# The recurrence's gates of a hybrid layer on one Trainium2 core: 128-row products one tile at a time, and 64-row products two tiles at a time

## The chip, the core and the metric

The kernel runs on one core of a Trainium2 chip. The metric is the device time of one execution in microseconds. The core's engines have their own instruction queues, each worked off in order: PE (TensorE) multiplies, ACT (ScalarE) evaluates functions, DVE (VectorE) does the elementwise work, POOL (GpSimd) a little of it, and SP (SyncE) issues most transfers. They meet only through semaphores.

## What is computed

The reference is one layer with three token mixers beside each other, for 512 positions of width 1024 in float32: a gated MLP (branch A), sparse attention with compressed keys (branch B) and a gated linear recurrence (branch C). The change is about branch C, about the projection that B's compression reads, and about the order in which gates of the merge are made.

```python
xc = conv4(xr) + conv_b                       # causal, per channel
xh = xc.reshape(B, S, 16, 64)                 # 16 heads of 64 channels
r = sigmoid(einsum('bshi,hio->bsho', xh, w_a) + b_a)
i = sigmoid(einsum('bshi,hio->bsho', xh, w_x) + b_x)
log_a = -8 * r * softplus(-lam)
a = exp(log_a)
b_in = sqrt(-expm1(2 * log_a)) * (i * xc)
h[t] = a[t] * h[t-1] + b_in[t]                # scan over positions
y_c = h * gelu(gate)
...
merged = g0 * (y_a @ w_br_a) + g1 * (y_b @ w_br_b) + g2 * (y_c @ w_br_c)
```

Everything behind (output projection, two norms, a SwiGLU block) is the same in both kernels.

## The kernel before

**Tiles.** Activations lie transposed, channels on the 128 partitions and the 512 positions along the row. A tile is 128 output channels of a projection. Float32 accuracy comes from halves: `split` (L131 on ACT, L136 on DVE) writes a rounded copy `hi` and then the rest `lo = x - hi`, and a product is hi*hi + hi*lo + lo*hi. A projection tile is thus 8 blocks of channels x 3 = 24 matmuls of 128x512 into one PSUM bank (`passes`, L263); a `yield` after each six lets other work be placed between them.

**Weights.** `wload` brings the weights of a tile through two raw buffers and has them split, in the order of `wlist`. The split of a coming tile is issued as the current one starts, so it stands on ACT and DVE between whatever else these two engines have in their queues; PE waits for it if it is late.

**Branch C.** `xr_tile(b, c)` (L488) makes one of two batches of four tiles: the projection, the convolution (L499 and L501, `xc`), the halves `ch` and `cl` of `xc`, and then the gates: for each of R and I three matmuls of 128x512 (L509), against block-diagonal weights `wab` that hold two heads of 64 channels, in a bank of the kind "tr". ACT reads R with a sigmoid (L511) and I with a tanh (L514), 128x512 each, and DVE makes (tanh + 1) * xc of it (L515). PSUM has six banks "mm" and two "tr". Once the four tiles of a batch are there, `rec_batch(b)` (L517) takes a tanh of R per tile (L523, T), one square root over the four (L524), four exponentials (L530), and per tile two multiplications on DVE (L539, L540) and the scan (L542). Sigmoid and tanh, root, and exponential lie in different tables of ACT, hence the two ACT_TABLE_LOAD of a batch. `rg_tile` makes the gelu gate of a tile (L451 to L454), `rec_out` (L556 and on) multiplies it in and splits the result into `ych` and `ycl`.

**The rest of the stretch.** `cmp_tile` makes the keys and values that B compresses, `compress` multiplies them (L784 first, then L800 or L814, with the tanh L793 between), `gate_tile` (L712 to L722) makes B's 48 gates and transposes them, and `c_gate(j)` (L1179) is a projection tile with a tanh for the merge of branch C. `c_stage` makes that merge: sums of y_c are split (the tiles named t, L131 and L136), and `b_pair` multiplies halves of weights and sums (L1273, 128x256 each), with its partial results copied out of the banks by ACT.

**What sets the order.** The work is written as generators. `run(main, side, rate)` steps through the tiles of `main` and advances `side` at the given rate; what a tile yields as a number is how many steps later its rest (the gates, say) is continued, in the list `late`. A scheduler places instructions on each engine in about this order, and `tc.issue_after(x)` keeps an instruction behind x. Around the change the main order is: the value tiles and compression tile 0; four input tiles of the first batch and the gate tile; four gelu tiles, compression tile 1 and four input tiles of the second batch, with the first batch's recurrence beside them; then a gelu tile (as fifth of the list), three more, compression tiles 2 and 3, branch gate 0, the first compression, branch gate 1, with the second batch beside them; then `c_stage`.

Of the kernel before, what the change touches and what calls it, by code (L numbers as in the profile page):

```python
# [52 lines left out]
def hybrid_block(ctx: ExitStack, tc: tile.TileContext, A, out):  # L53
# [89 lines left out]
    def w_in(*tiles):  # L143
# [5 lines left out]
    w_in(*range(T_XR + 1, T_XR + 8, 2), T_CMP + 1, *range(T_XR + 8, T_XR + 16, 2), *range(T_XR + 9, T_XR + 16, 2),  # L149
         T_CMP + 2, T_CMP + 3)  # L150
# [306 lines left out]
    wab = {}  # L457

# [5 lines left out]
    def load_wab():  # L464
        raw = wab["raw"]
        hi = slab("wabh", F32R, "wab", (2, NK, 128), 48)
        lo = slab("wabl", F32R, "wab", (2, NK, 128), 48)
        wab["hi"], wab["lo"] = hi, lo
        for _ in range(4):
            yield  # L470
        for k in range(0, NK, 2):
            split(raw[:, :, k:k + 2], hi[:, :, k:k + 2], lo[:, :, k:k + 2])
            yield
# [14 lines left out]
    def xr_tile(b, c):  # L488
        if c == 0:
            res["late"] = res["raw"]  # L490
            rec[b] = dict(R=slab("r", tag="y" if b else "m"), GG=slab("gg", tag="m"), TI=slab("ti", tag=("s0", "s1")[b]))
# [11 lines left out]
        ch, cl = row("ch", F32R), row("cl", F32R)  # L503
        split(xc, ch, cl)
        yield 4
        for g, dst in ((0, "R"), (1, "TI")):
            pg = bank("tr")
            for t, (w, x) in enumerate((("hi", ch), ("hi", cl), ("lo", ch))):
                PE.matmul(pg, wab[w][:, g, k, :], x, start=(t == 0), stop=(t == 2))  # L509
            if g == 0:  # L510
                SC.activation(rec[b]["R"][:, c, :], pg, AF.Sigmoid, bias=vec[:, V_BA + k:V_BA + k + 1])  # L511
            else:
                ti = rec[b]["TI"][:, c, :]
                last = SC.activation(ti, pg, AF.Tanh, scale=0.5, bias=half[:, 0, k:k + 1])  # L514
                res["ti"] = last, V.scalar_tensor_tensor(ti, ti, 1.0, xc, op0=OP.add, op1=OP.mult)  # L515
            yield

    def rec_batch(b):
        r = rec[b]
        r["T"] = slab("t", tag="s2")  # L520
        for c in range(4):
            k = 4 * b + c
            SC.activation(r["T"][:, c, :], r["R"][:, c, :], AF.Tanh, scale=sp4[:, k:k + 1])  # L523
        root = SC.activation(r["T"], r["T"], AF.Sqrt, scale=1.0 / 16)  # L524
# [182 lines left out]
    def gate_tile():  # L707
# [11 lines left out]
        yield  # L719
# [610 lines left out]
    def c_stage(first):  # L1330
# [20 lines left out]
        run([c_gate(2), hidden(second), c_gate(3)], begin(), 1.5)  # L1351
# [697 lines left out]
    def run(main, side=None, rate=1.0):  # L2049
# [3 lines left out]
        late = []  # L2053
# [212 lines left out]
```

## Time and profile before

| | us |
|---|---|
| median of 3 runs (1089.49 to 1089.56) | 1089.54 |
| the profiled execution | 1089.44 |
| its span, first to last instruction | 1087.7 |
| around the span | 1.74 |
| PE busy | 1078.3 (99%) |
| DVE busy | 883.0 (81%) |
| ACT busy | 661.7 (61%) |
| granted TensorE clock, mean | 0.998 |

PE is pipelined: a matmul of 128x512 is shown with 0.39 us, but the next one starts 0.227 us later, so start times count and not durations. On ACT and DVE, too, an instruction starts a little before the one ahead of it has ended. A row of the chain or of a timeline gives the start in the span, the length, the engine, and the line; "x4" stands for four in a row, and what is in square brackets is the idle time before it and what ended it. The stretch with the gate products lies between 66 and 147 us, the merge of branch C begins at 211 us.

### The profile page before, as it was taken

How to read it: one execution, taken by the hardware profiler on the slowest of the kernel's cores; microseconds unless marked ns; L12 is line 12 of the kernel's file. 1: busy time of each engine (PE TensorE's matmuls, PEld its weight loads, DVE VectorE, ACT ScalarE, POOL GpSimd, SP SyncE). 2: the span in 40 equal slices, each digit the busy share in tenths (PEclk: the TensorE clock that was granted, in tenths of full speed). 3: DMA queues.
4: the chain of work that ended last, by engine and by line, in shares of the span. 5: the costliest groups of instructions: out<-in, count | busy, mean ns of one | idle time of the engine just before them, and what ended most of it. 6: DMA issues, size and time to landing. Idle time of an engine off the chain costs nothing.

```text
span 1087.7 us, 16765 instructions
## 1 busy us (share of the span) xinstructions
PE 1078.3 (99%) x6450; PEld 948.5 (87%) x6450; DVE 883.0 (81%) x1557; ACT 661.7 (61%) x1210; POOL 29.0 (3%) x41
## 2 busy tenths in 40 slices
PE   9999999999999999999999999999999999999997
PEld 7888888999889888898888889988999999998886
DVE  6967779669675899998998887876988888889675
ACT  6757574454444676876777655555666666667542
POOL 0000000000000000000000000000000000022200
PEclk9999999999999999999999999999999999999999
DMA  8332325430322221102111134271323322378902
GB/s 312 113 99 82 97 86 204 178 98 20 117 78 78 78 59 39 59 20 79 59 39 59 58 118 136 72 257 39 117 78 117 117 104 97 130 227 202 191 20 97
DMA packets 35312, 115.07 MB, mean 106 GB/s; under 512 B 3584, under 2 KB 3984, under 8 KB 34336
## 3 DMA queue, kind: packets, MB, share of 16 engines
q1 hardware_dynamic: 28496, 97.01, 27.0%
q0 software_dynamic: 5152, 11.09, 5.0%
q10 hardware_dynamic: 1584, 5.90, 1.4%
q8 instruction: 50, 0.82, 0.3%
q14 instruction: 30, 0.25, 0.1%
HBM read 111.89 MB, written 2.10 MB: 105 GB/s over the span
## 4 chain that ended last, share of the span: by engine, by line
PE 97%; DVE 1%; DMA 0%; issue 0%; ACT 0%; DVEq 0%; SPq 0%; ACTq 0%
PE mm L263 37%; PE mm L1755 18%; PE mm L1273 7%; PE mm L1894 6%; PE mm L625 4%; PE mm L1509 4%; PE o L992 4%; PE sc L954 3%; PE tr L979 3%; PE tr L1894 3%; PE mm L870 2%; PE tr L784 1%; PE tr L509 1%; PE mm L1611 1%; PE tr L685 1%; PE tr L892 1%
## 5 line engine op out<-in xcount | busy, mean ns | idle before, releaser
L263 PE MATMUL mm<-hh,hi 128*128 128x512 f32 x504 | 199.5, 396 | 0.0
L263 PE MATMUL mm<-hh,lo 128*128 128x512 f32 x504 | 197.4, 392 | 0.0
L263 PE MATMUL mm<-hl,hi 128*128 128x512 f32 x504 | 196.9, 391 | 0.0
L136 DVE TENSOR_TENSOR lo<-raw,hi 128x1024 fp32r<-128x1024 f32 (+1 forms) x105 | 121.0, 1153 | 38.4 <-ACT hi L131 35.3
L131 ACT ACTIVATE hi<-raw 128x1024 fp32r<-128x1024 f32 (+1 forms) x105 | 105.3, 1003 | 46.5 <-PE mm L263 17.3
L263 PEld LDWEIGHTS mm<-hh,lo 128*128 128x128 f32 x504 | 94.6, 188 | 19.7
L263 PEld LDWEIGHTS mm<-hl,hi 128*128 128x128 f32 x504 | 94.7, 188 | 18.4 <-issue 0.2
L263 PEld LDWEIGHTS mm<-hh,hi 128*128 128x128 f32 x504 | 94.7, 188 | 18.0 <-PE mm L1273 0.2
L960 ACT ACTIVATE P<-P,ast 128x128 f32<-128x128 f32 (+3 forms) x128 | 70.7, 555 | 23.1 <-DVE ast L958 22.5
L958 DVE CUSTOM_DVE_ANT_0 P<-sc,mask 128x128 f32<-128x128 f32 (+3 forms) x128 | 57.9, 484 | 8.2 <-PE sc L954 7.3
L131 ACT ACTIVATE ph<-tr 128x512 fp32r<-128x512 f32 x80 | 46.9, 592 | 25.9 <-PE tr L979 24.0
L136 DVE TENSOR_TENSOR pl<-tr,ph 128x512 fp32r<-128x512 f32 x80 | 54.4, 685 | 2.7 <-PE o L992 0.9
L954 PE MATMUL sc<-K,q 128*128 128x512 f32 (+2 forms) x192 | 51.0, 368 | 0.0
L1755 PE MATMUL mm<-t,hi 128*128 128x256 f32 x288 | 50.7, 276 | 0.0
L1894 PE MATMUL mm<-hi,u 128*128 128x512 f32 x160 | 50.1, 389 | 0.0
L979 PE MATMUL tr<-ident,P 128*128 128x128 f32 x320 | 48.7, 273 | 0.0
L979 PEld LDWEIGHTS tr<-ident,P 128*128 128x128 f32 x320 | 39.0, 140 | 9.8 <-DVE pl L136 1.0
L136 DVE TENSOR_TENSOR lo<-bs,hi 128x1024 fp32r<-128x1024 f32 x28 | 34.1, 1220 | 11.6 <-ACT hi L131 11.6
L1755 PEld LDWEIGHTS mm<-t,hi 128*128 128x128 f32 x288 | 43.4, 188 | 0.0
L1755 PE MATMUL mm<-fh,hi 128*128 128x256 f32 x144 | 40.0, 278 | 0.0
L1755 PE MATMUL mm<-fh,lo 128*128 128x256 f32 x144 | 39.8, 276 | 0.0
L1755 PE MATMUL mm<-fl,hi 128*128 128x256 f32 x144 | 39.8, 276 | 0.0
(489 smaller groups left out, 2896.6 us busy)
## 6 DMA issues: line engine op xcount, KB each, us to landing
raw<-in_w_in SPq DMA_DIRECT2D x64, 512.0 KB, 3.5
rawp<-in_w_fi SPq DMA_DIRECT2D x20, 1024.0 KB, 5.1
bs<-in_w_fo POOLq DMA_DIRECT2D x20, 512.0 KB, 8.1
raw<-in_w_br SPq DMA_DIRECT2D x14, 512.0 KB, 3.6
w<-in_cw ACTq DMA_DIRECT2D x4, 1024.0 KB, 6.7
raw<-in_w_o SPq DMA_DIRECT2D x8, 512.0 KB, 4.1
bs<-in_w_fo SPq DMA_DIRECT2D x8, 512.0 KB, 8.0
raw<-in_w_v SPq DMA_DIRECT2D x6, 512.0 KB, 4.9
```

The costliest lines, as they stand in the source:

```text
L131: res["hi"] = SC.activation(hi, src, AF.Copy)
L136: res["lo"] = V.tensor_sub(lo, src, f32(hi))
L263: res["mm"] = PE.matmul(ps[:m, n0:n1], w[:, k * 128:k * 128 + m], x[k][:, n0:n1], start=(t == 0), stop=(t == 3 * NK - 1))
L625: res["mm"] = PE.matmul(b[c], x[k][:, c * 128:(c + 1) * 128], w[:, kk * 512:kk * 512 + 512], start=(k == 0 and t == 0), stop=(k == NK - 1 ...
L954: PE.matmul(ps[:, :w * n].rearrange("p (b n) -> p b n", b=w), lhs, K[:, i, brs[0]:brs[-1] + 1, :n], start=(i == 0), stop=(i == 1))
L958: V.tensor_tensor_reduce(out=t, in0=ps[:, b * n:b * n + n], in1=mask[0][:, S - n:], scale=-0.125, scalar=3.0e38, op0=OP.add, op1=OP.min, a ...
L960: SC.activation(t, t, AF.Exp, scale=-1.0, bias=st[:, 0, j, b:b + 1], accum_out=st[:, 1, j, b:b + 1])
L979: PE.transpose(pt[:, j * 128:(j + 1) * 128], self.part(j, br)[:, kt * 128:(kt + 1) * 128], ident)
L992: PE.matmul(po, VV[:, kt, g % 2, br].rearrange("p i d -> p (i d)"), x, start=(br == 0 and kt == 0 and t == 0), stop=(br == 1 and kt == a a ...
L1273: res["mm"] = PE.matmul(ps, u[:, k * 128:k * 128 + 128], v[:, k], start=(start and k == t == 0), stop=(k == 3 and t == 2), skip_group_chec ...
L1755: res["mm"] = PE.matmul(ps, w[:, k * 128:k * 128 + 128], x[:, k], start=(start and k == t == 0), stop=(k == 3 and t == 2), skip_group_chec ...
L1894: PE.matmul(ps, a, b, start=id(ps) not in begun, stop=i == len(ops) - 1, skip_group_check=True)
```

## The change

**Weights of the gates.** `load_wab` now lays `wab` out as, for each tile and each half of 64 partitions, 64 columns of R's head and 64 of I's. One matmul of 64 rows and 128 columns makes R and I of one head: R's 64 channels in the bank's rows 0 to 63, I's in rows 64 to 127.

**Two tiles at a time.** `xr_tile` leaves the gates to the second tile of each pair (c odd). Four banks "mm" are taken, one for each tile and half. In three rounds (hi*ch, lo*ch, hi*cl) four matmuls follow each other (L519), the pair's second tile first, the two halves in turn; they are held in this order with `issue_after`. That is 12 matmuls of 64 rows for a pair, 48 in all, as many as before. ACT reads each bank in 64x512: four sigmoids (L525) and four tanhs (L526) for a pair, where it was two and two of 128x512. The rows `ch` and `cl` use buffers of other kinds.

**Second pair of a batch.** After its sigmoids come the tanhs of T (L535, L536), the tanhs of the first tile's I, and then `rec_batch` is begun: the root (L550), then the exponentials (L556). The last tile's two tanhs of I are kept behind the root by `issue_after`. The list `late` is handed from one `run` to the next, so that the second pair's gates stand within the first tiles of the next stage; `gated` lets the recurrence wait for both pairs.

**Order of tiles.** Compression tile 2 moves ahead, to the end of the second batch's input tiles, and the gelu tiles of that batch follow all four together; the list of weights is changed to match. Branch gates 0 and 1 stand ahead of the first compression, gates 2 and 3 ahead of the second, where one of the two stood between. `gate_tile` continues its transposes two steps later.

The core of the diff:

```diff
@@ -148,4 +148,4 @@
     wlist.append((A["w_gate"], "gate"))
-    w_in(*range(T_XR + 1, T_XR + 8, 2), T_CMP + 1, *range(T_XR + 8, T_XR + 16, 2), *range(T_XR + 9, T_XR + 16, 2),
-         T_CMP + 2, T_CMP + 3)
+    w_in(*range(T_XR + 1, T_XR + 8, 2), T_CMP + 1, *range(T_XR + 8, T_XR + 16, 2), T_CMP + 2, *range(T_XR + 9, T_XR + 16, 2),
+         T_CMP + 3)
 
@@ -457,2 +457,3 @@
     wab = {}
+    ends = slice(0, 64), slice(64, 128)
 
@@ -465,4 +466,4 @@
         raw = wab["raw"]
-        hi = slab("wabh", F32R, "wab", (2, NK, 128), 48)
-        lo = slab("wabl", F32R, "wab", (2, NK, 128), 48)
+        hi = slab("wabh", F32R, "wab", (NK, 128), 48)
+        lo = slab("wabl", F32R, "wab", (NK, 128), 48)
         wab["hi"], wab["lo"] = hi, lo
@@ -470,5 +471,7 @@
             yield
-        for k in range(0, NK, 2):
-            split(raw[:, :, k:k + 2], hi[:, :, k:k + 2], lo[:, :, k:k + 2])
-            yield
+        for o in ends:
+            for i in range(2):
+                g = slice(64 * i, 64 * i + 64)
+                split(raw[o, i, :, o], hi[o, :, g], lo[o, :, g])
+                yield
 
@@ -490,3 +493,3 @@
             res["late"] = res["raw"]
-            rec[b] = dict(R=slab("r", tag="y" if b else "m"), GG=slab("gg", tag="m"), TI=slab("ti", tag=("s0", "s1")[b]))
+            rec[b] = dict(gates=0, R=slab("r", tag="y" if b else "m"), GG=slab("gg", tag="m"), TI=slab("ti", tag=("s0", "s1")[b]))
         k = 4 * b + c
@@ -502,16 +505,43 @@
         yield
-        ch, cl = row("ch", F32R), row("cl", F32R)
+        ch, cl = row("ch", F32R, "tg"), row("cl", F32R, "q32")
         split(xc, ch, cl)
-        yield 4
-        for g, dst in ((0, "R"), (1, "TI")):
-            pg = bank("tr")
-            for t, (w, x) in enumerate((("hi", ch), ("hi", cl), ("lo", ch))):
-                PE.matmul(pg, wab[w][:, g, k, :], x, start=(t == 0), stop=(t == 2))
-            if g == 0:
-                SC.activation(rec[b]["R"][:, c, :], pg, AF.Sigmoid, bias=vec[:, V_BA + k:V_BA + k + 1])
-            else:
-                ti = rec[b]["TI"][:, c, :]
-                last = SC.activation(ti, pg, AF.Tanh, scale=0.5, bias=half[:, 0, k:k + 1])
-                res["ti"] = last, V.scalar_tensor_tensor(ti, ti, 1.0, xc, op0=OP.add, op1=OP.mult)
-            yield
+        rec[b]["x"] = rec[b].get("x", []) + [(k, xc, ch, cl)]
+        yield 5 if c == 3 else 3
+        if c % 2 == 0:
+            return
+        two = rec[b].pop("x")
+        pg = [[bank("mm") for _ in ends] for _ in two]
+        for t in range(3):
+            for i, (k, xc, ch, cl) in reversed([*enumerate(two)]):
+                w, x = (("hi", ch), ("lo", ch), ("hi", cl))[t]
+                for n, own in enumerate(ends):
+                    with tc.issue_after(res["gate"].ins) if t or n or not i else nullcontext():
+                        res["gate"] = PE.matmul(pg[i][n], wab[w][own, k, :], x[own], start=(t == 0), stop=(t == 2))
+        yield
+        r = rec[b]
+
+        def act(out, part, k, own, n):
+            if part == 0:
+                return SC.activation(out[own], n[:64], AF.Sigmoid, bias=vec[own, V_BA + k:V_BA + k + 1])
+            return SC.activation(out[own], n[64:], AF.Tanh, scale=0.5, bias=half[own, 0, k:k + 1])
+
+        for i, (k, xc, ch, cl) in enumerate(two):
+            for n, own in enumerate(ends):
+                act(r["R"][:, k % 4, :], 0, k, own, pg[i][n])
+            if c == 3:
+                if i == 0:
+                    r["T"] = slab("t", tag="s2")
+                    for j in range(2):
+                        SC.activation(r["T"][:, j, :], r["R"][:, j, :], AF.Tanh, scale=sp4[:, 4 * b + j:4 * b + j + 1])
+                SC.activation(r["T"][:, k % 4, :], r["R"][:, k % 4, :], AF.Tanh, scale=sp4[:, k:k + 1])
+        for i, (k, xc, ch, cl) in enumerate(two):
+            ti = r["TI"][:, k % 4, :]
+            for n, own in enumerate(ends):
+                with tc.issue_after(r["root"].ins) if "root" in r else nullcontext():
+                    last = act(ti, 1, k, own, pg[i][n])
+            res["ti"] = last, V.scalar_tensor_tensor(ti, ti, 1.0, xc, op0=OP.add, op1=OP.mult)
+            if c == 3 and i == 0:
+                r["rec"] = rec_batch(b)
+                next(r["rec"])
+        r["gates"] += 1
 
@@ -519,7 +549,3 @@
         r = rec[b]
-        r["T"] = slab("t", tag="s2")
-        for c in range(4):
-            k = 4 * b + c
-            SC.activation(r["T"][:, c, :], r["R"][:, c, :], AF.Tanh, scale=sp4[:, k:k + 1])
-        root = SC.activation(r["T"], r["T"], AF.Sqrt, scale=1.0 / 16)
+        root = r["root"] = SC.activation(r["T"], r["T"], AF.Sqrt, scale=1.0 / 16)
 
@@ -718,3 +744,3 @@
         SC.activation(s[:64], s[:64], AF.Sigmoid)
-        yield
+        yield 2
         pt = bank("tr")
@@ -1350,3 +1376,3 @@
 
-        run([c_gate(2), hidden(second), c_gate(3)], begin(), 1.5)
+        run([c_gate(2), c_gate(3), hidden(second)], begin(), 1.5)
         more = seq(second, gmlp_prep(), v_norm())
@@ -2048,3 +2074,3 @@
 
-    def run(main, side=None, rate=1.0):
+    def run(main, side=None, rate=1.0, late=None, keep=False):
 
@@ -2052,3 +2078,3 @@
         credit = 0.0
-        late = []
+        late = late or []
         for m in main:
@@ -2069,4 +2095,4 @@
             credit += rate
-        for _, m in late:
-            for _ in m:
+        while late and not keep:
+            for _ in late.pop(0)[1]:
                 pass
@@ -2075,2 +2101,3 @@
                 pass
+        return late
 
@@ -2124,12 +2151,16 @@
     run([v_half(0), v_half(1), cmp_tile(0)], seq(norm(), load_wab()))
-    run(xr_tiles(0, gate_tile()))
-    tiles = xr_tiles(1, rg_tile(1, 0))
-    run(four(rg_tile, 0) + [cmp_tile(1)] + tiles[:4], rec_batch(0), 0.45)
+    late = run(xr_tiles(0, gate_tile()), keep=True)
+    tiles = xr_tiles(1, cmp_tile(2))
+
+    def gated(b):
+
+        while rec[b]["gates"] < 2:
+            yield
+        yield from rec[b]["rec"]
+
+    late = run(four(rg_tile, 0) + [cmp_tile(1)] + tiles[:4], gated(0), 0.45, late, True)
     def both_out():
 
-        batch = rec_batch(1)
-        next(batch)
-        yield
-        yield from after(res["ti"], rec_out(0))
-        yield from batch
+        yield from after((res["cv"],), rec_out(0))
+        yield from gated(1)
         yield from rec_out(1)
@@ -2144,5 +2175,5 @@
 
-    run([tiles[4], *(rg_tile(1, c) for c in range(1, 4)), cmp_tile(2), inputs(cmp_tile(3), 0),
-         behind(c_gate(0), "x0", "x1"), hidden(first), inputs(c_gate(1), 1)],
-        both_out(), 0.45)
+    run([tiles[4], *four(rg_tile, 1), inputs(cmp_tile(3), 0),
+         c_gate(0), behind(c_gate(1), "x0", "x1"), inputs(hidden(first), 1)],
+        both_out(), 0.45, late)
     c_stage(first)
```

What this does to the order of instructions is shown at three places. In a row, numbers behind a name tell apart the tiles of that name.

ACT from the last input gates of the first batch to the next weights, before: r is R (and later a), t is T, ti is I, gs a gelu tile's row, hi the rounded half of the weights for the fourth gelu tile.

```order
L511 ACTIVATE r_631<-tr_860,vec 128x512
L523 ACTIVATE t_896<-r_631,sp_96 128x512
L514 ACTIVATE ti_633<-tr_865,half 128x512
L524 ACT_TABLE_LOAD
L524 ACTIVATE t_896<-t_896 128x2048
L530 ACT_TABLE_LOAD
L530 ACTIVATE r_631<-r_631,spm_97 128x512 x4
L451 ACTIVATE gs_912<-mm_871 128x512
L131 ACTIVATE hi_920<-raw_918 128x1024
```

And after, from the last of the four sigmoids of the second pair:

```order
L525 ACTIVATE r_631<-mm_868,vec 64x512
L536 ACTIVATE t_889<-r_631,sp_96 128x512 x2
L526 ACTIVATE ti_633<-mm_865,half 64x512
L526 ACTIVATE ti_633<-mm_866,half 64x512
L550 ACT_TABLE_LOAD
L550 ACTIVATE t_889<-t_889 128x2048
L556 ACT_TABLE_LOAD
L556 ACTIVATE r_631<-r_631,spm_97 128x512 x4
L526 ACTIVATE ti_633<-mm_867,half 64x512
L526 ACTIVATE ti_633<-mm_868,half 64x512
L451 ACTIVATE gs_915<-mm_846 128x512
L131 ACTIVATE hi_923<-raw_921 128x1024
```

Ahead of the root stand eight instructions of the pair, where three of one tile stood, and two reads of 64 rows have come between the exponentials and the split.

DVE in the same stretch, before, from the last input product to the lo half of the same weights:

```order
L515 SCALAR_TENSOR_TENSOR ti_633<-ti_633,xc_806 128x512
L539 SCALAR_TENSOR_TENSOR t_896<-r_631,t_896 128x512 x2
L540 TENSOR_TENSOR t_896<-t_896,ti_633 128x512 x2
L452 SCALAR_TENSOR_TENSOR gs_912<-gs_912,mm_871 128x512
L542 SCALAR_TENSOR_TENSOR ti_633<-r_631,t_896 128x512
L136 TENSOR_TENSOR lo_921<-raw_918,hi_920 128x1024
```

And after:

```order
L565 SCALAR_TENSOR_TENSOR t_889<-r_631,t_889 128x512 x2
L566 TENSOR_TENSOR t_889<-t_889,ti_633 128x512 x2
L568 SCALAR_TENSOR_TENSOR ti_633<-r_631,t_889 128x512
L542 SCALAR_TENSOR_TENSOR ti_633<-ti_633,xc_810 128x512
L452 SCALAR_TENSOR_TENSOR gs_915<-gs_915,mm_846 128x512
L568 SCALAR_TENSOR_TENSOR ti_633<-r_631,t_889 128x512
L136 TENSOR_TENSOR lo_924<-raw_921,hi_923 128x1024
```

A second scan (L568; L542 before) and the last input product (L542; L515 before) have moved in between the first exponential and the lo half. The second batch has the like, with an output half in place of one scan.

PE where the branch products begin (c_stage), before: the end of branch gate 3, then the first products.

```order
L263 MATMUL mm_1789<-hl_136,hi_1629 128x512
L263 MATMUL mm_1789<-hh_134,lo_1630 128x512
L1273 MATMUL mm_1815<-ych_1336,hi_1714 128x256
L1273 MATMUL mm_1815<-ycl_1337,hi_1714 128x256
L1273 MATMUL mm_1815<-ych_1336,lo_1715 128x256
```

And after: the end of the second compression, then the products.

```order
L810 MATMUL tr_1772<-x_247_1680,w_244_1674 128x124 x8
L810 MATMUL tr_1772<-xcmp_593,w_245_1675 128x124 x8
L1299 MATMUL mm_1831<-ych_1294,hi_1731 128x256
L1299 MATMUL mm_1831<-ycl_1295,hi_1731 128x256
L1299 MATMUL mm_1831<-ych_1294,lo_1732 128x256
```

The 24 matmuls of the third branch gate have gone from between the compression and the products.

## The prediction

> **What bounds the kernel now.** I read the page first, then the chain of waits, then the timelines of three engines.
>
> ```profile
> PE 1078.3 (99%) x6450; PEld 948.5 (87%) x6450; DVE 883.0 (81%) x1557; ACT 661.7 (61%) x1210; POOL 29.0 (3%) x41
> PE 97%; DVE 1%; DMA 0%; issue 0%; ACT 0%; DVEq 0%; SPq 0%; ACTq 0%
> ```
>
> PE (the matmul engine) is the kernel: 97% of the chain, and no transfer has a share. Two things alone move the end: a shorter PE program, or a wait of PE that was not there. The chain of waits, cut to where the gate products (L509) stand, shows the program as pieces (start, length, count):
>
> ```profile
> 66.93 1.36 PE tr L509 x6
> 68.29 5.44 PE mm L263 x24
> 80.53 1.36 PE tr L509 x6
> 81.89 3.63 PE mm L712 x16
> 85.51 2.27 PE mm L263 x10
> 89.95 35.59 PE mm L263 x157
> ```
>
> A product of 512 columns costs 1.36 / 6 = 5.44 / 24 = 0.227 us, and PE never pauses. Eight tiles of six gate products are 48 x 0.227 = 10.88 us. That is the most that the change touches, 1% of the span.
>
> **The gate products in halves.** There are still 48, each on 64 rows of the weights and of the operand, in 24 pairs, one on rows 0-63 and the next on rows 64-127. If a pair takes the time of one, 24 x 0.227 = 5.44 us go; if the halves run one after another, nothing goes. The trace has one place with a 64-row operand, the transposes of the gate tile:
>
> ```profile
> 87.39 0.39 PE L263 MATMUL mm<-hh,hi 128*128 128x512 f32 x1
> 87.71 0.46 PE L722 MATMUL tr<-ident,gsig 64*128 64x64 f32 x4
> 88.10 0.50 PE L509 MATMUL tr<-ch,wabh 128*128 128x512 f32 x1
> 88.43 0.39 PE L509 MATMUL tr<-cl,wabh 128*128 128x512 f32 x1
> ```
>
> All four use the same rows, so they cannot show whether two halves overlap. They do show the edges: from 87.39 to 87.71 and from 88.10 to 88.43 are 0.32 and 0.33 us where 0.227 is usual, 0.1 us for going into the form and 0.1 for leaving it. Four groups make 8 x 0.1 = 0.8 us; the bounds are 0 and 0.8, and I take 0.8, since both edges show it. I take the overlap as whole, for the rows of a pair share nothing: -5.44 + 0.8 = -4.6 us.
>
> The Trainium skill ("TensorE: Matmul & The Clock Gate", Part 3: Packing small matmuls, Measured speedup vs the span model) gives 3.07 times for four packed row tiles, not 4. By an estimate at that same share, 0.77, the pairs save 3.8 us here instead of 5.4, and the sum below would be about 1.6 us higher. No run here shows the packed form yet.
>
> **Who reads the results.** Each tile's R and I now lie in two banks by halves, so ACT reads four times 64x512 where it read twice 128x512: 32 reads for 16. The timeline of ACT, first the only 64x512 read of a bank in before, then the first batch:
>
> ```profile
> 85.55 0.60 ACT L716 ACTIVATE gsig<-mm 64x512 f32<-64x512 f32 x1 [0.97 <-PE mm L712]
> 86.05 1.05 ACT L131 ACTIVATE hi<-raw 128x1024 fp32r<-128x1024 f32 x1
> 89.08 0.69 ACT L511 ACTIVATE r<-tr,vec 128x512 f32<-128x512 f32 x1 [1.47 <-PE tr L509]
> 89.81 0.72 ACT L523 ACTIVATE t<-r,sp 128x512 f32<-128x512 f32 x1
> 90.44 0.67 ACT L514 ACTIVATE ti<-tr,half 128x512 f32<-128x512 f32 x1
> 91.13 1.28 ACT L524 ACT_TABLE_LOAD   x1
> 92.42 1.92 ACT L524 ACTIVATE t<-t 128x2048 f32<-128x2048 f32 x1
> 94.34 1.28 ACT L530 ACT_TABLE_LOAD   x1
> 95.64 2.56 ACT L530 ACTIVATE r<-r,spm 128x512 f32<-128x512 f32 x4
> 98.11 0.57 ACT L451 ACTIVATE gs<-mm 128x512 f32<-128x512 f32 x1
> 98.59 1.05 ACT L131 ACTIVATE hi<-raw 128x1024 fp32r<-128x1024 f32 x1
> ...
> 145.62 0.69 ACT L511 ACTIVATE r<-tr,vec 128x512 f32<-128x512 f32 x1 [2.43 <-PE tr L509]
> 146.21 0.68 ACT L514 ACTIVATE ti<-tr,half 128x512 f32<-128x512 f32 x1
> ```
>
> Half the rows are not half the time: 0.60 beside 0.69, and the next instruction starts 0.50 later, or 0.59 behind the full form. I take 0.58 with 0.50 as the lower bound. ACT has 39% of its time free, so the 16 more reads cost nothing as such. They cost where ACT's queue is in order and PE waits for what stands behind: the hi half (L131) and then DVE's lo half (L136) of the next weights.
>
> The Trainium skill ("TensorEngine Tiling (Array Packing)", Performance Considerations, PSUM Bottleneck) says that tiling makes the matmuls faster but not the emptying of their banks, which can become the limit. By that rule the readers give the gain back, as places 1 and 2 price it from rows; a sum without those two would be -2.4 us. The rows above agree with its premise, 0.60 for half the rows.
>
> **Place 1, the first batch.** Here the readers of the last pair, root and exponentials come in one piece. DVE in before:
>
> ```profile
> 96.40 1.30 DVE L539 SCALAR_TENSOR_TENSOR t<-r,t 128x512 f32<-128x512 f32 x2 [4.56 <-ACT r L530]
> 97.62 1.29 DVE L540 TENSOR_TENSOR t<-t,ti 128x512 f32<-128x512 f32 x2
> 98.82 0.68 DVE L452 SCALAR_TENSOR_TENSOR gs<-gs,mm 128x512 f32<-128x512 f32 x1
> 99.42 1.22 DVE L542 TENSOR_TENSOR_SCAN ti<-r,t 128x512 f32<-128x512 f32 x1
> 100.55 1.20 DVE L136 TENSOR_TENSOR lo<-raw,hi 128x1024 fp32r<-128x1024 f32 x1
> ```
>
> That lo is done at 101.75. Its tile is 61 products behind 89.95, and its third product, the first to read lo, starts at 89.95 + 63 x 0.227 = 104.2: 2.5 us of slack. After, in the clock of before: the first pair's products take 1.36 for 2.72, so the fourth input tile ends at 80.53 - 1.36 = 79.2; gate tile 3.63 and half a tile (12 products) 2.72 bring the second pair to 85.5 and its end to 86.9. ACT then runs four sigmoids, two tanhs for T and two for I, 8 x 0.58 = 4.6, to 91.5; table 1.28, root 1.92, table 1.28, to 96.0; the first exponential (2.56 / 4) to 96.6. DVE waits for that, then runs the pair L565/L566 twice (96.40 to 98.82: 2.42), a scan (99.42 to 100.55: 1.13), the last input product L542 and the gelu's step (0.6 each), the second scan 1.13, and lo 1.20: 7.1 us, so lo at 103.7. Before had one scan ahead of it; now there are two scans and a product. PE wants it at 104.2 - 2.72 = 101.5. PE waits 2.2 us; with the edges, which shift both sides, 2.3. Bounds: 0.50 a read makes ACT 0.6 shorter, so 1.6; a wait for hi as well makes 2.7.
>
> **Place 2, the second batch,** counted from the end C of compression tile 2, which now stands ahead of the pair. PE runs one tile 5.44, the gates 1.36 and two tiles 10.88, and two products of the fifth: lo is wanted at C + 18.1. ACT is held by ych, the halves of the first batch's output (0.35 each, below), until C + 5.3; then 4.6 for the eight and 4.5 for table, root, table, and the first exponential: C + 15.1. DVE then has L565 twice, L566, L542, an output half, the gelu's step, a scan and lo: 1.2 + 0.6 + 0.6 + 0.4 + 0.6 + 1.13 + 1.20 = 5.7, C + 20.8.
>
> ```profile
> 155.56 0.76 DVE L136 TENSOR_TENSOR ycl<-ti,ych 128x256 fp32r<-128x256 f32 x2
> ```
>
> The wait is 2.7; bounds 1.5 (shorter reads, and ych done sooner) and 3.3.
>
> **Place 3, the merge of branch C.** In before the third branch gate's 24 products stand between the compression (L784) and the branch products (L1273). After, that gate runs earlier, and the products follow the compression at once. The chain, ACT and DVE:
>
> ```profile
> 199.55 6.45 PE tr L784 x56
> 206.00 5.48 PE mm L263 x24
> 211.48 9.57 PE mm L1273 x84
> ...
> 204.25 2.01 ACT L131 ACTIVATE t<-ti 128x1024 fp32r<-128x1024 f32 x2 [3.16 <-PE tr L784]
> 206.60 1.06 ACT L131 ACTIVATE t<-ti 128x1024 fp32r<-128x1024 f32 x1
> 207.56 1.05 ACT L131 ACTIVATE hi<-raw 128x1024 fp32r<-128x1024 f32 x1
> 211.83 0.40 ACT L793 ACTIVATE chid<-chid 128x248 f32<-128x248 f32 x1
> ...
> 209.36 1.22 DVE L136 TENSOR_TENSOR lo<-raw,hi 128x1024 fp32r<-128x1024 f32 x1
> ```
>
> The splits of the sums t begin when compression frees their slab, 204.25, 1.75 us ahead of its end, and the last hi ends at 208.61, lo at 210.58. In before that was over as the products began at 211.48. After, with S the end of compression (206.00 here), products start at S. Fifteen of them (9.57 / 84 = 0.114 each) reach the first that reads hi at S + 1.7; hi is there at S + 2.6: 0.9 us. The bank of the first product is wanted again, and its copy stands on ACT behind hi and one more 128x512 split (half of 1.05 or so): 0.7 more. The next copy stands behind the tanh of the hidden tile: 0.4. Together 2.0 us. Bounds: 0.5 if only hi is late and the splits start sooner, 3.5 if lo at S + 4.6 and the copies add up.
>
> **Edits at nothing.** The weights of the gates are split in as many pieces as before, under the first tiles. Compression tile 2 and two branch gates move with their loads (SP) and readers; loads run two tiles ahead, and the chain has 0% DMA; without that cover a load's late landing would cost up to 1 us, which the upper end holds. Tile by tile banks become four at a time of six; a bank late by a read would be 0.6. I allow 0.2 for these. The exponentials' tables are loaded as often as before.
>
> **Sum.** -4.6 + 2.3 + 2.7 + 2.0 + 0.2 = +2.6 us. The profiled execution took 1089.44 us, span 1087.7 and 1.74 around it; the median of the runs is 0.10 higher, 1089.54. So 1092.1 us.
>
> **Rivals.** First, the halves do not overlap, and the change doesn't shorten PE's program at all: the edges cost 0.8. PE then wants the late weights up to 2.7 us later while ACT also starts 1.4 later, so place 2 falls to some 1.4 and place 1 stays near 2: 0.8 + 2.1 + 1.4 + 2.0 = +6.3, 1095.8. For it speaks only that no row shows an overlap. Second, no measurable difference: reads at 0.50 (places 1 and 2 at 1.6 and 2.0), and place 3 at its low end 0.5, give -4.6 + 4.3 = -0.3, 1089.2. Third, on the other side, one mechanism: the chain of ACT ahead of the first exponential. If a read of 64 rows costs half of one of 128, 0.3 us, the six reads ahead of the root give back 1.7 us in each batch, and places 1 and 2 fall to 0.6 and 1.0. With place 3 at 1.0 that is -4.6 + 2.6 = -2.0, and -2.8 if the edges cost nothing: 1086.7 to 1087.5. It turns the sign when the three waits together fall below 4.6 us. The row of 0.60 for 64x512 speaks against it. With no waits at all it would be 1084.
>
> **Chances.** The forecast 0.55 (its own range 1090.3 to 1094.5), no overlap 0.13, no difference 0.18, faster chain 0.14. About 0.2%, 2.2 us, is what a measurement of this kernel can tell from no change, so the bounds are 1087.4 and 1091.7. Of the forecast's 0.55 some 0.15 lies under 1091.7, and of the second rival 0.03 lies under 1087.4: faster 0.17, same 0.30, slower 0.53. The range, 1087.4 to 1095.8, takes in the forecast, both middle cases and the serial halves, and leaves out most of the third rival.
>
> **What would show it.** In the profile after: the gate products (L519) at 0.113 us apiece if they overlap, 0.227 if not; gaps of PE with DVE or ACT as releaser at an L263 tile soon after each batch's exponentials, 2 to 3 us each, with lo (L136) behind two scans; and a gap of some 2 us in the products (L1299) with ACT as releaser. I am wrong if the gate products are short and the chain stays whole at those three places, or if the 64-row reads are well under 0.5 us.

## The result and the profile after

The changed kernel takes 1098.66 us, the median of six runs from 1097.94 to 1100.45, beside 1089.75 for the kernel before: a ratio of 1.0082 (95% interval 1.0069 to 1.0095), 8.9 us slower. The direction is the one forecast; the size is more than three times it (8.9 us for 2.6), above the upper end of the range, 1095.8. The profiled execution took 1099.83 us, with a span of 1098.1, 10.4 more than before. It is one of the longer ones: the spans of the six go from 1096.2 us at a mean granted clock of 0.997 to 1098.8 at 0.994. First the page's line of engines, then what PE waited for between 60 and 240 us, of the changed kernel:

```profile
PE 1081.0 (98%) x6450; PEld 946.5 (86%) x6450; DVE 885.0 (81%) x1557; ACT 674.6 (61%) x1226; POOL 29.0 (3%) x41
```

```profile
PE mm L263 <- DVE lo L136: 3.4, 3, 1.6
PE mm L263 <- ACT hi L131: 3.2, 2, 2.4
PE mm L1299 <- ACT hi L131: 0.9, 1, 0.9
PE mm L1299 <- ACT r L1307: 0.4, 1, 0.4
PE mm L1299 <- ACT r L1303: 0.3, 1, 0.3
```

In before the same view is empty. From 254 us on, the starts of later stages stand 10.4 to 10.5 us behind those of before, so all of it arises in the stretch that the change touches.

**The gates.** PE's timeline at the first pair (L519):

```profile
70.65 0.39 PE L263 MATMUL mm<-hh,lo 128*128 128x512 f32 x1
70.97 0.74 PE L519 MATMUL mm<-ch,wabh 64*128 64x512 f32 x4
71.54 0.63 PE L519 MATMUL mm<-ch,wabl 64*128 64x512 f32 x4
72.00 0.64 PE L519 MATMUL mm<-cl,wabh 64*128 64x512 f32 x4
72.56 0.50 PE L263 MATMUL mm<-hh,hi 128*128 128x512 f32 x1
72.90 0.40 PE L263 MATMUL mm<-hl,hi 128*128 128x512 f32 x1
```

Four products take 0.46 us (71.54 to 72.00), two pairs of 0.23: the halves overlap wholly. The edges cost twice what was priced: 0.57 for the first round, 0.56 for the last, and 0.32 and 0.34 for the neighbouring products. A group adds 72.90 - 70.65 - 2 x 0.227 = 1.80 us where 12 products of 128 rows took 2.72, so four groups save 3.7 us.

**Place 1.** ACT and DVE from the second pair's reads to the next weights, answering to the rows of the first batch in before:

```profile
87.39 2.53 ACT L525 ACTIVATE r<-mm,vec 64x512 f32<-64x512 f32 x4
89.94 1.34 ACT L536 ACTIVATE t<-r,sp 128x512 f32<-128x512 f32 x2
91.31 1.40 ACT L526 ACTIVATE ti<-mm,half 64x512 f32<-64x512 f32 x2
92.72 1.28 ACT L550 ACT_TABLE_LOAD   x1
...
97.24 2.56 ACT L556 ACTIVATE r<-r,spm 128x512 f32<-128x512 f32 x4
99.70 1.37 ACT L526 ACTIVATE ti<-mm,half 64x512 f32<-64x512 f32 x2
...
101.72 1.06 ACT L131 ACTIVATE hi<-raw 128x1024 fp32r<-128x1024 f32 x1
```

```profile
97.99 1.31 DVE L565 SCALAR_TENSOR_TENSOR t<-r,t 128x512 f32<-128x512 f32 x2 [3.88 <-ACT r L556]
...
100.42 1.22 DVE L568 TENSOR_TENSOR_SCAN ti<-r,t 128x512 f32<-128x512 f32 x1
...
102.73 1.22 DVE L568 TENSOR_TENSOR_SCAN ti<-r,t 128x512 f32<-128x512 f32 x1
103.87 1.20 DVE L136 TENSOR_TENSOR lo<-raw,hi 128x1024 fp32r<-128x1024 f32 x1
```

The queue is the one that was forecast, row by row; the eight instructions ahead of the root take 5.3 us (87.39 to 92.72), not 4.6: a 64-row read costs 0.63 to 0.70 when the next is like it, and a tanh of T 0.69. PE there:

```profile
102.83 0.50 PE L263 MATMUL mm<-hh,hi 128*128 128x512 f32 x1 [0.81 <-ACT hi L131]
103.17 0.40 PE L263 MATMUL mm<-hl,hi 128*128 128x512 f32 x1
105.12 0.80 PE L263 MATMUL mm<-hh,lo 128*128 128x512 f32 x1 [1.55 <-DVE lo L136]
105.71 0.63 PE L263 MATMUL mm<-hh,hi 128*128 128x512 f32 x1
106.14 0.63 PE L263 MATMUL mm<-hl,hi 128*128 128x512 f32 x1
```

By start times PE loses 0.96 and 1.72 us, 2.7 in all. And then something that the prediction did not have: products start 0.43 us apart instead of 0.227. The windows show the granted clock (the figure behind POOL's):

```profile
102.00:105.00 3.00, 0.76 (x3) 0.30 (x2) 3.00 (x5) 3.00 (x5) 0.00 (x0) 1.00 0.00 0
105.00:109.00 4.00, 3.88 (x10) 3.15 (x11) 4.00 (x7) 0.85 (x2) 0.00 (x0) 0.57 0.55 151
...
166.00:169.00 3.00, 0.74 (x3) 0.30 (x3) 3.00 (x4) 3.00 (x6) 0.00 (x0) 1.00 0.00 0
169.00:174.00 5.00, 5.00 (x15) 3.97 (x16) 5.00 (x8) 3.07 (x6) 0.00 (x0) 0.66 0.63 211
```

After each of the two long waits the clock is halved for some 3 us (0.50 from 105.01 to 108.42 and from 169.87 to 173.28); by start times that costs 1.6 us at each place.

**Place 2.** ACT ahead of the second batch's last reads, then DVE in the same stretch and PE at the weights that came late:

```profile
148.94 0.44 ACT L131 ACTIVATE ych<-ti 128x256 fp32r<-128x256 f32 x1
...
151.88 0.42 ACT L131 ACTIVATE ych<-ti 128x256 fp32r<-128x256 f32 x1 [2.50 <-DVE ti L584]
152.32 2.10 ACT L525 ACTIVATE r<-mm,vec 64x512 f32<-64x512 f32 x3
```

```profile
149.85 1.27 DVE L776 COPY xcmp<-mm 64x256 f32<-64x256 f32 x2
151.15 1.90 DVE L584 TENSOR_TENSOR ti<-ti,gg 128x512 f32<-128x512 f32 x3
```

```profile
166.97 0.50 PE L263 MATMUL mm<-hh,hi 128*128 128x512 f32 x1 [2.44 <-ACT hi L131]
...
169.00 0.50 PE L263 MATMUL mm<-hh,lo 128*128 128x512 f32 x1 [1.29 <-DVE lo L136]
```

The gates had been ready since 149.3; ACT's in-order queue stood still for 2.5 us at an output half that waited for DVE, which was at the copies of compression tile 2 (xcmp, 149.85 to 151.1). By start times PE's wait came out at 2.60 for hi and 1.46 for lo, 4.1 us. Place 3 cost 2.0 us in the products (L1299) and 0.7 at lo of the branch gate behind them.

Together: -3.7 for the gates, waits of 2.7 + 4.1 + 2.7 = 9.5, half speed 3.2: 9.0. The other 1.4 of this execution's 10.4 are small: the first product after a wait takes 0.11 us more at each of eight places, 0.9 together, and I did not follow the rest.

### The profile page after: what moved, and what is told of

The parts are those of the page before. It is cut to its first block, busy times and chain, and to the rows that moved or that the text cites. A ratio compares the mean times of both kernels' runs of the same rounds, so it can differ in the third digit from the quotient of the medians.

```text
span 1098.1 us, 16794 instructions
## 1 busy us (share of the span) xinstructions
PE 1081.0 (98%) x6450; PEld 946.5 (86%) x6450; DVE 885.0 (81%) x1557; ACT 674.6 (61%) x1226; POOL 29.0 (3%) x41
## 4 chain that ended last, share of the span: by engine, by line
PE 92%; ACT 3%; DVE 3%; DMA 1%; issue 0%; DVEq 0%; ACTq 0%
PE mm L263 33%; PE mm L1781 17%; PE mm L1920 6%; PE mm L1299 6%; PE mm L651 4%; PE mm L1535 4%; PE o L1018 4%; PE sc L980 3%; PE tr L1005 3%; PE tr L1920 3%; PE mm L896 2%; PE tr L810 1%; PE mm L1637 1%; DMA raw<-in_w_in 1%; PE tr L711 1%; PE tr L918 1%
## 5 line engine op out<-in xcount | busy, mean ns | idle before, releaser
L263 PE MATMUL mm<-hh,hi 128*128 128x512 f32 x504 | 201.8, 400 | 3.2 <-ACT hi L131 3.2
```

What stands on the lines that cost most here:

```text
L263: res["mm"] = PE.matmul(ps[:m, n0:n1], w[:, k * 128:k * 128 + m], x[k][:, n0:n1], start=(t == 0), stop=(t == 3 * NK - 1))
```

## The experiments

Twelve kernels, each timed beside the kernel before; medians, and the ratio to before with its interval.

### Undoing half of the order of branch gates: e1_gate3_between

```diff
-        run([c_gate(2), c_gate(3), hidden(second)], begin(), 1.5)
+        run([c_gate(2), hidden(second), c_gate(3)], begin(), 1.5)
```

> The changed kernel with the order in c_stage undone: branch gate 2, second compression, branch gate 3. Theory W (three places where PE waits, the third of them between compression and branch products): in the profile after, the first four groups of branch products took 12.46 us for 9.57 of before and the branch gate behind them 0.9 more, so 2.9 to 3.8 us come back, about 1095.3 us against 1098.7. Rival: the merge is held by its loads and splits whatever stands ahead, and the wait only moves behind branch gate 3: under 1 us comes back.

1098.18 us, 1.0075 (1.0058 to 1.0093): the rival. The products' waits shrank, and the branch gate behind them waited for hi twice instead. Its profiled execution showed how far the clock's part varies: the same waits as the changed kernel's at place 1, but 14 half-speed products where that had 8, 3.0 us lost for 1.6.

```profile
104.00:109.00 5.00, 4.36 (x10) 3.51 (x11) 5.00 (x8) 1.36 (x3) 0.00 (x0) 0.50 0.50 147
```

### lo products last in the gelu tiles: e2_lo_last

```diff
     def rg_tile(b, c):
...
-        yield from matrix(ps, hh, hl)
+        hi, lo = unit()
+        ops = [(w, x, k) for k in range(NK) for w, x in ((hi, hh), (hi, hl))] + [(lo, hh, k) for k in range(NK)]
```

> The changed kernel with the 24 products of a gelu tile in another order: first the 16 that read the hi half of the weights, then the 8 that read lo. So lo is wanted 14 products, 3.2 us, later; hi as before. Theory W with a clock that drops after a wait of some length: at place 1 the 1.7 us for lo go and 0.9 for hi stay, too short to drop the clock, so the 1.7 us of half-speed products go as well: -3.4; at place 2 the 1.5 us for lo go and 2.6 for hi stay; with the drop there -1.5, without it -3.0. Sum -4.9 to -6.4, 1092.3 to 1093.8 us. Rival: the half-speed stretch does not come from the wait but from the gate form or from the transfers that run at the time; then only 3.2 us come back, 1095.5.

1094.55 us, 1.0038 (1.0028 to 1.0047), 4.1 us under the changed kernel. The time lies between the two forecasts. Both waits for lo are gone; place 1 keeps 1.0 us for hi and shows no half speed, place 2 keeps 2.8 for hi and does, as theory W had it. The waits are the weights' splits.

### Products that do nothing in place of the waits: e3_filler

```diff
     def rg_tile(b, c):
         ps = bank("mm")
+        if c == 3:
+            for n in range((12, 18)[b]):
+                PE.matmul(ps, hh[n % NK][:, :128], hl[n % NK], start=True, stop=True)
```

> The changed kernel with products that do nothing (their bank is written anew by the tile) put ahead of the two gelu tiles that wait: 12 of 128x512 (2.7 us) at place 1, 18 (4.1 us) at place 2, as long as the waits seen there. Theory W with the clock drop caused by the idle PE: the tiles start as late as before, but at full clock, so the 1.7 to 1.9 us of half-speed products in each place go: -3.4, 1095.3 us. Rival: the clock drops for another reason (transfers, the form of the gates): no change, 1098.7, half-speed products still there, or slower by what the fillers overrun.

1096.80 us, 1.0057 (1.0042 to 1.0072), between the two forecasts. The waits at places 1 and 2 are filled, and the clock stays up, with as many transfers under way as in the changed kernel or more (DMA shares of 0.59 and 0.90 for 0.55 and 0.63):

```profile
105.00:109.00 4.00, 4.00 (x18) 3.01 (x17) 4.00 (x7) 1.25 (x3) 0.00 (x0) 1.00 0.59 145
...
169.00:174.00 5.00, 5.00 (x23) 4.13 (x22) 5.00 (x8) 3.08 (x6) 0.00 (x0) 1.00 0.90 297
```

So the clock drops because PE stands idle. Against the changed kernel 3.3 us came back between the two profiled executions, 1.9 between the medians: not every execution pays the whole of it.

### One half, then the other: e4_one_half_then_other

```diff
-        for t in range(3):
+        for at, t in ((n, t) for n in range(2) for t in range(3)):
             for i, (k, xc, ch, cl) in reversed([*enumerate(two)]):
...
-                for n, own in enumerate(ends):
+                for n in (at,):
+                    own = ends[n]
```

> The changed kernel with the same 48 gate products, but in each group first the six of rows 0-63 and then the six of rows 64-127, so that neighbours share their rows. Theory that two neighbours on different rows run at once: a group takes 12 x 0.227 = 2.72 us for the 1.6 of the changed kernel, four groups +4.4 us, of which the waits at places 1 and 2 (2.7 and 4.1 us) can take back up to half, since PE then comes later: 1100.9 to 1103. Rival: what made the group short is the 64 rows and not the neighbour: 1.6 us a group and no change, 1098.7.

1095.05 us, 1.0048 (1.0029 to 1.0067): faster than the changed kernel, which neither side had. The group itself did get longer, 2.25 us (70.50 to 72.75) for 1.59. It is not twice as long, because PE began the second half's products beside the first's:

```profile
71.52 0.39 PE L520 MATMUL mm<-ch,wabh 64*128 64x512 f32 x1
71.53 0.39 PE L520 MATMUL mm<-cl,wabh 64*128 64x512 f32 x1
...
71.76 0.39 PE L520 MATMUL mm<-cl,wabh 64*128 64x512 f32 x1
```

Within one half the starts still lie 0.21 to 0.24 us apart (71.53 and 71.76), so 64 rows alone make no product shorter; what shortens the group is that products on different rows run beside each other.

What went was elsewhere. The scheduler placed two products of the first batch's output (L585) ahead of the copies on DVE, so ACT did not stand still and place 2 fell from 4.1 us to 0.3, and at place 1 2.1 us of waits did not halve the clock. As a test of the overlap the run was confounded; e11 repeats it without the waits.

### All branch gates back, and the whole order of tiles back: e5_c_gates_back, e6_tile_order_back

```diff
 e5 and e6:
-        run([c_gate(2), c_gate(3), hidden(second)], begin(), 1.5)
+        run([c_gate(2), hidden(second), c_gate(3)], begin(), 1.5)
-         c_gate(0), behind(c_gate(1), "x0", "x1"), inputs(hidden(first), 1)],
+         behind(c_gate(0), "x0", "x1"), hidden(first), inputs(c_gate(1), 1)],
 e6 besides (and the list of weights to match):
-    tiles = xr_tiles(1, cmp_tile(2))
+    tiles = xr_tiles(1, rg_tile(1, 0))
-    run([tiles[4], *four(rg_tile, 1), inputs(cmp_tile(3), 0),
+    run([tiles[4], *(rg_tile(1, c) for c in range(1, 4)), cmp_tile(2), inputs(cmp_tile(3), 0),
```

> The changed kernel with all four branch gates of the c stage where they stood before (gate 0, first compression, gates 1 and 2, second compression, gate 3). Theory W: place 3's waits (2.0 us in the products, 0.7 in the branch gate behind them) go with the gate that was moved ahead of the first compression, which undoing half of the move did not show: -2.7, about 1096.0 us. Rival: the merge of branch C waits for the sums of y_c, which come late because of place 2; then the waits stay near 2.3 us and the time at 1098.2.

> The changed kernel with the whole order of tiles of before (compression tile 2 behind the gelu tiles again as well), so that what stays of the change are the 64-row pairs, the second pair carried over and the root ahead of the last input gates. Theory: the 4.1 us at place 2 and the half speed behind them come from compression tile 2, whose copies (xcmp) on ACT and DVE stand ahead of the products of the first batch's output and so held ACT idle for 2.5 us ahead of the gates' reads; then place 2 falls to 1.5 us or less with no half speed, place 3 is gone, place 1 stays at 2.7 and 1.6: 1098.7 - 4.1 - 2.7 = about 1092 us. Rival: place 2 is the length of the readers' chain alone; then only place 3 goes: 1096.

e5: 1097.29 us, 1.0072 (1.0057 to 1.0087); e6: 1096.26, 1.0057 (1.0042 to 1.0072). e5 lies between its two forecasts: the products no longer wait, as theory W had it, but the first compression waits 1.1 us for its inputs (x). e6 has the time of its rival by another sum: place 2 falls to 2.9 us, not to 1.5, and keeps its half speed (1.5 us), so the copies of compression tile 2 are part of it and the readers' chain is the rest. The first compression waits 1.6. Place 1 is 2.7 us in both profiled executions, with no half speed behind it; in e6:

```profile
106.00:110.00 4.00, 3.84 (x17) 3.20 (x18) 4.00 (x7) 0.88 (x2) 0.00 (x0) 1.00 0.63 158
```

### The pairs alone: e7_pairs_alone

The kernel before with `load_wab` and the pairs of the change; `rec_batch`, `run` and the order of tiles are those of before.

```diff
-        yield 4
-        for g, dst in ((0, "R"), (1, "TI")):
...
+        yield 4
+        if c % 2 == 0:
+            return
+        two = rec[b].pop("x")
...
```

> The kernel before with the 64-row products in pairs of tiles, read in halves, and nothing else of the change: order of tiles, no carrying over, all input gates ahead of the root. Theory W: the gates give 4.4 us, the readers' chain in front of the first exponential of the first batch is as long as in the changed kernel or longer by two reads, so place 1 waits 2.7 us and runs 1.6 at half speed; place 2 some 1 us: 1089.7 - 4.4 + 4.3 + 1 = about 1090.6. Rival: the loss is in the carrying over and the root; then the pairs alone keep their gain, 1085.3.

1104.07 us, 1.0131 (1.0114 to 1.0149): worse than both sides expected. PE waits at the gates themselves, 8.4 us in two waits for `ch` of the pair's last tile (its split stands behind the reads of the pair before), and 3.3 us more far behind, at a gelu (L454), which I did not trace back. Half clock (6.8 and 3.4 us of it) stands at the longer of the two waits and at the gelu. Carrying the second pair over is thus not what costs; without it, in this form, the pairs cost more.

### Both repairs: e8_order_back_lo_last

e6 with the edit of e2.

> The kernel of e6_tile_order_back with the lo products of the gelu tiles last (as in e2_lo_last): lo is wanted 3.2 us later. Theory W: place 1 keeps 1.0 us for hi, too short for half speed, place 2 keeps at most what hi lacks, 0 to 1 us: 1089.7 - 4.4 + 1 to 2 = 1086.3 to 1087.3, under both kernels. Rival: a wait moves to the next tile, whose weights are split behind the same queue, and 2 to 3 us come back: 1089 to 1090.

1093.69 us, 1.0035 (1.0021 to 1.0048): the rival's mechanism, at 4 us more than it gave. Place 2 now lies at compression tile 2, which is no gelu tile and so still takes lo third: waits of 1.3 and 1.5, half speed (a clock of 0.66 from 164 to 169), and the compression's 1.6.

### The root two steps later: e9_root_two_steps_later, e10_changed_root_later

e9 is e6, and e10 the changed kernel, each with this edit in `xr_tile`:

```diff
             if c == 3 and i == 0:
+                for _ in range(2):
+                    yield
                 r["rec"] = rec_batch(b)
```

> The kernel of e6_tile_order_back with one edit: between the first reads of a second pair and the root stand two steps of the main work (12 products), so that the split of the next gelu tile's weights comes ahead of root and exponentials on ACT and ahead of the scans on DVE. Nothing is left out and nothing runs faster. Theory W: the waits at places 1 and 2 (2.7 and 2.9 us in e6, half speed of 1.5 behind the second) are gone, the gates' gain of 4.2 stays, and what is left is the first compression's wait of 1.6 for its inputs: 1089.7 - 4.2 + 1.6 = 1087.1 us, under both kernels. Rival: the chain of the recurrence is long whatever stands ahead of it, and the root that comes later makes the sums of y_c and the outputs late: the waits move behind the second batch, and the time stays at 1093 to 1096.

> The changed kernel itself with the same edit alone (order of tiles as changed). Theory W: places 1 and 2 lose their 6.7 us of waits and the 3.4 us at half speed; a wait of 2 us for lo comes in behind place 2, where the second scans now stand, and place 3 keeps its 2.7: 1098.7 - 10.1 + 2 = 1090.6 us. Rival: as in e9, no change to speak of: 1097 to 1099.

e9: 1089.75 us in eleven runs, 0.9999 (0.9990 to 1.0008). e10: 1093.62, 1.0030 (1.0018 to 1.0042), 5.0 us under the changed kernel by a delay of two steps. Both lie between their two forecasts. ACT in e9, to be held against the changed kernel's first batch:

```profile
91.12 1.40 ACT L526 ACTIVATE ti<-mm,half 64x512 f32<-64x512 f32 x2
92.55 0.60 ACT L451 ACTIVATE gs<-mm 128x512 f32<-128x512 f32 x1
93.17 1.06 ACT L131 ACTIVATE hi<-raw 128x1024 fp32r<-128x1024 f32 x1
94.25 1.28 ACT L552 ACT_TABLE_LOAD   x1
```

hi is done at 94.2 instead of 102.8, and PE waits at neither place. One wait is left, at the first compression:

```profile
PE tr L812 <- DVE x L793: 2.1, 1, 2.1
```

The gates' 3.7 us less 2.3 lost there should show as 1.4; the profiled span is 1.0 shorter than that of before, the medians are equal. The granted clock goes with the difference: the six executions of e9 with a mean of 0.998 or 0.999 have spans of 1086.4 to 1088.0 us (median 1086.8), the five with 0.996 or 0.997 of 1087.8 to 1088.7, and before, timed beside them, has a median of 1088.1. So where the clock held, 1.3 us of the gain show; that the others lost it in half clock behind the one wait, as e11 below does, is likely, but no trace shows them. In e10, waits of 1.2 and 1.8 us come in one tile behind place 2, and place 3 is as it was.

### The overlap without the waits: e11_root_later_serial_halves

e9 with the order of e4's gate products.

> The kernel of e9_root_two_steps_later with the gate products in the order of e4 (six of one half, then six of the other). Theory that neighbours on different rows run at once: with no long wait to hide it a group takes 2.25 us (as in e4) for 1.6, four groups +2.6, and the compression's wait may grow by up to 2 as the inputs come later: 1089.7 to 1091.7 us beside 1087.1 of e9. Rival: the overlap is worth nothing in the sum, as e4's time might suggest: the same time as e9.

1095.03 us, 1.0047 (1.0033 to 1.0061), 5.3 us over e9, more than either side had. The groups take some 0.8 us more each, 3 together; the compression's wait grows from 2.3 to 4.2, and half speed follows it (a clock of 0.50 from 183 to 187). The overlap is real and worth some 3 us of PE's program; the rest is again a wait and its sequel.

### The order alone: e12_order_alone

The kernel before with the tile order of the change and nothing else of it.

> The kernel before with the changed order of tiles alone (compression tile 2 behind the second batch's input tiles, branch gates 0 and 1 ahead of the first compression, 2 and 3 ahead of the second); gates as 128-row products, recurrence as before. Theory W: place 3 is a matter of this order and of nothing else in the change, so PE waits 2.0 us in the first branch products and 0.7 in the branch gate behind them, and nowhere else: 1089.9 + 2.7 = 1092.6 us. Rival: place 3 came from the sums of y_c being late in the changed kernel (a sequel of place 2); then the order alone costs nothing: 1089.9.

1092.85 us, 1.0027 (1.0018 to 1.0037), 3.2 us slower than before. The waits of PE, all of them those of place 3:

```profile
PE mm L1273 <- ACT hi L131: 0.9, 1, 0.9
PE mm L1273 <- ACT r L1281: 0.4, 1, 0.4
PE mm L263 <- DVE lo L136: 0.3, 1, 0.3
PE mm L1273 <- ACT r L1277: 0.3, 1, 0.3
```

So place 3 belongs to the order and to no sequel of place 2.

## Why the prediction was too small

- **The gates in halves:** right in kind (whole overlap), 3.7 us for 4.6. The edges were priced at 0.2 us a group from the transposes; a group of products has 0.4, with the first and last round. The Trainium skill's share of 0.77 ("TensorE: Matmul & The Clock Gate", Part 3: Packing small matmuls, Measured speedup vs the span model) would have given 3.8 for the four groups, before any edges; inside a group the trace shows 0.46 us for two pairs, a share of 1, and the loss at the edges.
- **Place 1:** right, 2.7 us for 2.3, the upper bound given for a wait for hi as well. The mis-sized term is the row of eight instructions ahead of the root: the 64-row reads took 0.63 to 0.70 us and T's tanhs 0.69, for 0.58.
- **Place 2:** right mechanism, wrong size, 4.1 for 2.7. From the end of compression tile 2 (C, by the count of products at 146.3) ACT began at C + 6.0, not 5.3; its eight instructions took 5.5 us, not 4.6 to 4.7; DVE needed 6.0 from the first exponential to lo, not 5.7; and PE came 0.5 later, with the edges. ACT's stop was in the forecast as the hold by ych, but the move of the tile, which brings the copies there, was entered at nothing: e6, with the tile back, has 2.9 us.
- **Place 3:** right, 2.0 us in the products for 2.0; and 0.7 in the branch gate behind them where 0.2 had been allowed for everything unnamed. e12 shows it by itself.
- **The step that failed is the sum.** It had no term for what a wait leaves behind: after an idle stretch of PE the next products run at half clock. It cost 1.6 us at each of two places in the profiled execution, and 1.9 to 3.3 in all by e3. That is the largest part of the miss but not the whole of it. In the profiled execution 7.8 us are missing (10.4 for 2.6): half clock 3.2, place 2 1.4, the gates' edges 0.9, place 3 with the branch gate behind it 0.5, place 1 0.4, and the 1.4 that belong to none of these. Without half clock the time would still lie above the range: e3 has none, with the waits filled, and took 1096.80.

  The granted clock of before could show it only at its very end: it is 1.00 in every window up to 1083 us and 0.50 from there on, 3 us behind PE's last product (1080.1), where nothing is left to be slowed. The Trainium skill describes such a drop ("TensorE: Matmul & The Clock Gate", Part 1: The HAM clock gate): half rate after an idle window of some 3.4 us, in windows that run freely. I should have weighed that rule. The runs agree with it in part: the halving is there, in stretches of 3.4 us or twice that, but waits of 2.7 us together, with two products between them, were enough in the changed kernel and e1, while the same waits in e5 and e6 left the clock alone.
- **The rival that the halves do not overlap** (1095.8) was nearest in time, for a reason that is not there. The rival with a faster chain fell with the price of the 64-row read. Its "1084 with no waits at all" comes out only if the edges cost nothing; with its own -4.6 it is 1085.

That the waits with their sequels are the loss is shown: e2 takes lo out, e3 takes out the half clock, e9 takes out places 1 and 2 by order alone, and e12 adds place 3 by order alone. Why the gain does not show in full even then is read from traces, around e9's one wait. First before, then e9: the root of the second batch, the compression's input x, and in e9 the compression.

```profile
149.76 1.92 ACT L524 ACTIVATE t<-t 128x2048 f32<-128x2048 f32 x1
...
176.31 1.21 DVE L765 TENSOR_TENSOR x<-xcmp,cpe 128x1024 f32<-128x1024 f32 x1
```

```profile
156.04 1.92 ACT L552 ACTIVATE t<-t 128x2048 f32<-128x2048 f32 x1
...
179.97 1.22 DVE L793 TENSOR_TENSOR x<-xcmp,cpe 128x1024 f32<-128x1024 f32 x1
...
181.24 2.05 PE L812 MATMUL tr<-x,w 128*128 128x124 f32 x16 [2.12 <-DVE x L793]
```

PE is free for the compression at 179.0 us, 0.9 sooner than it began in before (179.9), since twelve more products stand ahead of it in e9. The input is there 3.7 us later (181.2 for 177.5). The root begins 6.3 us later: the eight instructions of the second pair take 5.5 us (146.45 to 151.92) where the last tile's three took 1.8 (145.62 to 147.40), and the two steps put more between them and the root. DVE stands idle for 3.8 and 3.9 us meanwhile, waiting for ACT, and is full from the first exponential on (19.87 of 20 us from 162 to 182), so it does not make the lateness good. Which part each of the three has, the longer readers' chain, the two steps and the full DVE, is argued, not shown: no run separates them.

## What to carry to other kernels

Where one engine is 99% busy, shortening its program moves the deadlines of all that feeds it forward; go through the in-order queues of the other engines for what is due next, above all at a batch whose instructions come in one piece, and put the due piece (here one split of weights) ahead of the batch: two steps of delay were worth 5 us in e10. Price a wait of the matmul engine with its sequel, here 1.6 us or, in e1, 3.0 us of half clock behind some 3 us of idling, and expect it to differ from one execution to the next. A tile that is moved brings its readers' copies along, on every engine that they use.

## What was not expected of the hardware

- The clock's drop depends on more than the wait's length: with 0.96 and 1.72 us of waits at the same place, 0 (e5, e6), 8 (changed kernel) and 14 (e1) half-speed products followed. Wherever half clock ends within the kernel, it has lasted 3.41 us or twice that, and its beginnings in one trace lie whole multiples of 3.41 us apart (105.01 and 169.87 in the changed kernel: 19 of them; 143.70 and 338.26 in e7: 57). So the clock seems to go by windows that run on whatever PE does, and what counts is how a wait falls into them: of 101.60 to 105.01, the window ahead of the drop, PE was busy 1.16 us in the changed kernel; in e6 the same wait is spread over two windows, 102.04 to 105.45 with 1.75 us and the next with 2.70, and nothing dropped. No single busy time divides all cases (1.49 us left the clock alone in e7, 1.70 halved it in e1).
- With the halves in sequence, PE ran products of the second half beside those of the first (starts 0.01 to 0.02 us apart in e4), so a group took 2.25 us and not 2.72.
- A read of 64x512 from a bank by ACT takes 0.63 (sigmoid) to 0.70 us (tanh) in a row of its like; a tanh of 128x512 in such a row took 0.69, and behind a read of 128x512 in before the next instruction started 0.48 to 0.73 us later, by what it was. Half the rows bought no time.
